# Attention value products with the transposed probabilities as stationary operand

## The chip, the cores and the metric

The kernel runs on one core of one Trainium2 chip. It is one launch, and the metric is the device time of that launch in microseconds (us). Five engines work in it, each through its own instruction queue in a fixed order: TensorE (PE; its weight loads are listed as PEld), VectorE (DVE), ScalarE (ACT), GpSimd (POOL) and SyncE (SP), which issues most of the DMA transfers.

## The reference, cut to what matters

The program is one inference step of a hybrid backbone with two layers, on 512 latent and 128 context tokens of 1024 features. Layer 0 mixes tokens with attention and RWKV-7 side by side, layer 1 with an S5 state space model; a SwiGLU stands before and after each mixer. The change touches attention alone, which computes for 8 query heads in 2 groups (one key and value head for each four of them), 64 features per head:

```python
def one_block(qblk):                     # 128 queries
    sc = jnp.einsum('bqkgd,btkd->bkgqt', qblk, k).astype(F32) * scale
    p = jax.nn.softmax(sc, axis=-1).astype(v.dtype)
    return jnp.einsum('bkgqt,btkd->bqkgd', p, v)
```

Latent queries read 640 keys (512 latent, 128 cached), context queries the 128 context keys.

## The kernel before, in words

Activations lie feature-major: features on partitions, tokens beside them. The five sub-layers outside the mixer of layer 0 do not change. In that mixer the input projection comes first, then the stage in question (`rwkv_attention`, L665), then the output projection (from L605 on).

In the stage four RWKV units of two heads each run one after the other: preparation (`rwkv_prep`, L939), inversion of triangular systems (`tri_inverse`), the chain of states from chunk to chunk (`rwkv_chain`, L1042) and the output (`rwkv_out`, L1140). They are generators; `take` (L679) draws from those of neighbouring units in turn and spreads 40 blocks of attention among them, so that the blocks fill gaps. This sets the order in which the program is written. A scheduler then orders the instructions of each engine by its own estimate of their times, so the order on an engine is not quite the written one.

A step of a chain is, on PE, a first product and one that adds the state (L1086, L1097), a copy of the result by ACT and DVE to `rt` (L1099), a product with it (L1102), a copy to `uv` (L1104), the next state (L1110, read out by DVE in L1113), and beside it what the tokens read (`ps_yr`, L1121 and L1123).

A block of attention (`att_block`, L896) is one query head and 128 queries. Four pairs of heads, five blocks of queries and two heads make 40 blocks: 32 with 640 keys, 8 with 128. In order:

- L905, L906 or L908 (PE): scores, queries on partitions, in the two wide banks of PSUM.
- L911, L912 (DVE): the row maximum, and its product with the scale.
- L914 (ACT): exponential into `att_p`, with the row sums beside it; L915 (DVE): one over the row sums.
- L916 (ACT): the probabilities times that, in place.
- L923 (PE): transposes of 128 by 128, five or one, into one or two PSUM banks `pt`; L925 (ACT): copies to `pts`, now with keys on partitions.
- L929 (PE): the value products, summed over the key tiles into the first of these banks. The values (`vt`, 64 columns of a head) are stationary, `pts` moves: 128 columns. The result has 64 features on partitions and 128 queries beside them, as the output projection wants it.
- L930 (ACT): copy to half of `att_out`; after the second head of a pair SP stores both heads with one DMA to `od` (L893).

PSUM tiles with the tag `ps` (scores excepted) come from three banks, given out in program order; `pt`, `ps_yr`, `ps_A`, `ps_hs` and others share them. All these products are in float32, and PE issues each as two passes (a transpose is one), with a weight load before each pass.

Of the kernel before, what the change touches and what calls it, by code (L numbers as in the profile page):

```python
# [18 lines left out]
LAT = 512  # L19
# [5 lines left out]
# token columns: latent 0..511, context 512..639; half 0 = 0..319, half 1 = 320..639  # L25
SEGS = (((0, HALF, 0),), ((0, LAT - HALF, 0), (LAT - HALF, HALF, 1)))
# weights are split ahead of this many instructions
# [4 lines left out]
class K:  # L32
    """The network on one core. Activations are feature-major: [features, tokens]."""
# [22 lines left out]
    def open_psum(self):  # L56
        """tags of PSUM and their buffers; a tag's buffers are given out in program order."""
        self.psum, self.banks = self.open("psum", 1, space=PSUM), {"ps": 3, "pn": 2, "pb": 1}
        # two banks side by side, for the mixer, and two more of ps otherwise
        self.wide = self.psum.tile([128, 1024], F32, name="ps_wide")  # L60
        self.five, self.count = True, 0

    def open_res(self):
        """temporaries, weights raw and in two parts, input of the next product, residual."""
        self.small = self.open("small", 2, "right")
        self.wraw = self.open("wraw", 3, "right")
        self.whl = self.open("whl", 4, "right")
        self.act = self.open("act", 1, "right")
        self.res = self.open("res", 1, "right")

    def load(self, dst, src):
        """a load that the scheduler keeps behind the load before it."""
# [28 lines left out]
    def setup(self):  # L101
        """parameters and tokens; the loads that the first sub-layer waits for come first."""
# [11 lines left out]
            # these wait until the first sub-layer runs  # L114
# [7 lines left out]
        def rows_of(name):  # L122
            """rows of parameters ..."""
# [11 lines left out]
        def columns(name, rows):  # L135
            """... turned into one scalar per partition."""
# [26 lines left out]
        # silu of both condition vectors; 32 stationary columns, of which 2 are in use  # L163
# [15 lines left out]
        # tokens, feature-major  # L179
# [10 lines left out]
        # the first sub-layer's vectors and norms  # L190
        self.ada(0, 0, ())
        self.new_h()
        for t in range(4):
            if t == 3:
# [3 lines left out]
                # 1 + the bias of scale; gain of the output times the weight of the residual  # L198
# [40 lines left out]
    def ada(self, l, j, parts):  # L239
        """pieces of work that make mods[l, j][:, part, d, group]: shift, scale, gate of sub-layer j of layer l."""  # L240
# [13 lines left out]
    def ada_piece(self, l, j, part, t, w=None):  # L254
        """two of the eight input tiles; four groups of 256 outputs go to as many column groups of the array."""
# [24 lines left out]
        if part:  # L280
            # gain * (1 + scale), or weight * gate * gain
            g = self.par["npre" if part == 1 else "npost"][:, i0:i0 + KT]
            nc.gpsimd.tensor_tensor(m[:, part], m[:, part], g[:, :, None].to_broadcast([128, KT, 2]), op=OP.mult)

# [1 line left out]
    def spill_x(self):  # L286
        """keep the residual in DRAM while a mixer needs the room."""
# [27 lines left out]
    def rms_bcast(self, ss):  # L315
        """ss [128, HALF]: squares summed over the feature tiles -> 1/rms on all partitions (PSUM)."""
        nc = self.nc
        ps = self.ps("ps_ms", "pn")
        # three blocks of 128 tokens; the last one overlaps, and its upper half counts
# [13 lines left out]
    def pre_norm(self, l, j, half, rb):  # L333
        """modulated input of sub-layer j as two float32r parts."""
# [35 lines left out]
    def post_norm(self, l, j, half, y, ssy, stats=True):  # L370
        """x += gate * rms_norm(y) * gain; returns the squares of x, summed over the feature tiles."""
# [16 lines left out]
    def wload(self, src, kt, n):  # L388
        """src: DRAM [kt*128, n] -> raw tile [128, kt, n]."""
# [4 lines left out]
    def wsplit(self, w, kt, c0, eng=None):  # L394
        """128 columns of a raw weight tile as two float32r parts."""
# [9 lines left out]
    def early_weights(self, l, j, between=None):  # L405
        """the first weights of a sub-layer, ready before its input: raw tiles and tiles in parts."""
# [14 lines left out]
    def mm3(self, ps, whl, acts, half, kt, k0=0, k1=None):  # L421
        """ps[:, :HALF] = sum over k of w[k]^T a[k], three passes; the terms k0 .. k1 of them."""
# [9 lines left out]
    def flush(self):  # L432
        """the norm of the second half, behind the first products of the first half."""
# [8 lines left out]
    def ffn(self, l, j, on_half, fillers=(), bg=()):  # L442
        """y[d][half] = swiglu(h); on_half(half, squares) when a half is complete."""
# [31 lines left out]
        def background():  # L475
# [3 lines left out]
            # behind the norms at the sub-layer's start  # L479
# [5 lines left out]
        for bi, (f0, f1) in enumerate(FBLOCKS):  # L485
# [9 lines left out]
            # the first and the last block take one half after the other, so that the norms of one half run  # L495
            # beside the products of the other
# [34 lines left out]
    def ab(self, l, j, on_half, fillers):  # L531
# [10 lines left out]
        def in_weights(c0, eng=None):  # L542
            """columns c0..c0+127 of the input projection."""
# [6 lines left out]
        def q_weights(i):  # L550
            """query heads i and 4 + i."""
# [28 lines left out]
        # the first products run beside the norm of the second half  # L580
# [16 lines left out]
        # what the last unit's output needs, and above it what is free before: even units, chains, the rest  # L597
# [9 lines left out]
        # output projection; its rows are permuted as the attention heads are  # L607
# [11 lines left out]
        # the place of the residual, which comes back when all of this is split  # L619
# [21 lines left out]
        # four products wait for the last unit's features only  # L641
# [23 lines left out]
    def rwkv_attention(self):  # L665
        """the units in turn: the chain of one runs beside the preparation of the next, and attention
        fills the gaps."""
        att = self.attention()
        # factors of a chunk's columns: block diagonal in the two heads
# [3 lines left out]
        # right sides of the chains' systems, over rows of zeros  # L673
# [5 lines left out]
        def take(rounds, n, *gens):  # L679
            """all of the generators, evenly, with n blocks of attention spread over them."""  # L680
# [58 lines left out]
    def ab_take(self, kind, n, half, ps):  # L739
        """one half of 128 projected features."""  # L740
        nc, mix = self.nc, self.mix
        if kind == "rw":
            # centred shift mix: (1 - mu) p + mu/2 (left + right)
# [41 lines left out]
        # mean square per token and head, tokens on partitions -> 1/rms  # L785
# [11 lines left out]
    def head_rsqrt(self, sq, scale, eps, op, name, bufs=2):  # L797
        """sq [128 = 2 heads x 64, NT] -> (scale * sums over a head  op  eps) ** -0.5 as [token, 5, 2]."""
# [12 lines left out]
    def head_bcast(self, st):  # L811
        """[token, 5, 2] -> [2 heads x 64, NT] in PSUM: (columns, their part)."""
# [12 lines left out]
    def mm_sq(self, lhsT, rhs, name):  # L825
        """[128, NT] = lhsT^T rhs in float32, in PSUM: (columns, their part)."""
# [6 lines left out]
    def rope(self, src, dst):  # L833
        """dst[:, :LAT] = src rotated; both [128, >= LAT]."""
# [29 lines left out]
    def att_values(self, v):  # L864
        """values with tokens on partitions: 4 latent blocks, the context, the cache."""
# [11 lines left out]
    def attention(self):  # L877
        """query heads i (rows 0..63) and 4 + i (rows 64..127), 128 queries at a time."""
        nc, mix = self.nc, self.mix
        # of both heads, each with zeros in place of the other's rows: the array's rows are all in use  # L880
# [3 lines left out]
        for i in range(4):  # L884
# [3 lines left out]
            for qb in range(5):  # L888
                o = self.mixe.tile([128, 128], F32, name="att_out", bufs=2)
                for kv in range(2):  # L890
                    self.att_block(qs[kv], self.attr[i], o, qb, kv)
                    if kv:
                        nc.sync.dma_start(self.od[i][:, qb * 128:(qb + 1) * 128], o)  # L893
                    yield

    def att_block(self, q, r8, o, qb, kv):  # L896
# [19 lines left out]
        nc.scalar.activation(p[:, :nk], p[:, :nk], AF.Identity, scale=mx[:, 3:4])  # L916
# [9 lines left out]
        po = pt[0][rows, :128]  # L926
        blocks = [0, 1, 2, 3, 5] if lat else [4]
        for n, b in enumerate(blocks):
            nc.tensor.matmul(po, self.vt[:, b, rows], pts[:, n], start=(n == 0), stop=(n == nkt - 1))  # L929
        nc.scalar.copy(o[rows], po)  # L930

# [1 line left out]
    # Unit i: heads 2i and 2i + 1, both directions, in chunks of 64 tokens. The backward direction  # L933
    # is the forward one on the reversed tokens; its chunks 0, 1 are the context, 2..9 latent.
    # Each stage is a generator, so that the stages of neighbouring units and attention take turns.
# [3 lines left out]
    def rwkv_prep(self, i, u):  # L939
        """decays, scaled factors and the products inside the chunks."""  # L940
# [10 lines left out]
        # normalised key direction, halved  # L951
# [13 lines left out]
        for d in range(2):  # L965
# [3 lines left out]
            # log decay: c1 * (tanh(z / 2) + 1), cumulated inside each chunk  # L969
# [43 lines left out]
            # rows: b | k of token s, columns: a | r of token t; and b | k with tokens on partitions  # L1013
# [21 lines left out]
        # bonus  # L1035
# [6 lines left out]
    def rwkv_chain(self, i, u):  # L1042
        """the states, chunk after chunk: four latent streams, and the four context streams beside them."""
        nc, I, O, mix = self.nc, self.I, self.O, self.mix
        am, v, ec = u["am"], u["v"], u["ec"]
        # values, tokens on partitions 64..127: position 0..7 latent chunks, 8, 9 context, per direction
# [852 lines left out]
```

## Time and profile before

| | us |
|---|---|
| three runs | 3339.91, 3347.76, 3350.36 |
| median | 3347.76 |
| span of the profiled execution, first to last instruction | 3337.1 |
| median less span (what lies around the span) | 10.7 |
| PE, DVE, ACT, POOL busy | 3091.3, 1923.3, 1210.2, 683.2 |
| the stage with attention: 738 to 1350 us of the span | 612 |

The span is read first by its share of busy time and its chain of waits, then by stretches: the stage is 18% of it, and nothing outside it is touched.

### The profile page before, as it was taken

Reading aid. Unit: us, or ns where it says so; the run is one execution under the profiler, and the core shown is the slowest. Engines: PE = TensorE matmul, PEld = TensorE weight load, DVE = VectorE, ACT = ScalarE, POOL = GpSimd, SP = SyncE. Lnnn points to the kernel's source line nnn. Section 1 sums busy time; section 2 is a strip of 40 time slices with the busy share of each in tenths; the row PEclk is TensorE's granted clock in tenths of the full one; section 3 lists DMA queues with packets and bytes.
Section 4 is the critical chain, followed back from the end, with each engine's and each line's share of the span. In section 5 each row is a group of like instructions: output and inputs, shape, how many; then the busy total and the mean of one; then the engine's idle time right before and its main releaser. Section 6 shows DMA issues by size and latency. Waiting matters only on the chain.

```text
span 3337.1 us, 55197 instructions
## 1 busy us (share of the span) xinstructions
PE 3091.3 (93%) x22259; PEld 2857.2 (86%) x22259; DVE 1923.3 (58%) x3731; ACT 1210.2 (36%) x2491; POOL 683.2 (20%) x795
## 2 busy tenths in 40 slices
PE   7999999986789789899999999999997689999998
PEld 6999998974576567789999999999996579999998
DVE  5433357428735861475466686666487955733346
ACT  4422235325334432453332453233353235422223
POOL 1000014132001200153333231233142533100002
PEclk8999999987778796899999999999998789999998
DMA  6433245620000000735443445454358863342223
GB/s 223 153 101 127 99 136 183 220 84 17 5 21 15 13 7 3 199 109 159 142 153 122 155 137 167 138 165 142 115 139 204 272 204 120 108 139 76 76 89 108
DMA packets 333924, 404.44 MB, mean 121 GB/s; under 512 B 42217, under 2 KB 299174, under 8 KB 333414
## 3 DMA queue, kind: packets, MB, share of 16 engines
q1 hardware_dynamic: 319174, 361.96, 34.4%
q0 software_dynamic: 14496, 38.97, 3.9%
q8 instruction: 175, 2.87, 0.4%
q14 instruction: 79, 0.65, 0.1%
HBM read 356.79 MB, written 42.89 MB: 120 GB/s over the span
## 4 chain that ended last, share of the span: by engine, by line
PE 80%; DVE 10%; issue 3%; POOL 2%; DMA 2%; ACT 2%; SPq 0%; POOLq 0%; DVEq 0%; ACTq 0%
PE ps_h L428 9%; PE ps_h L429 9%; PE ps_h L430 9%; PE ps_wide L428 5%; PE ps_wide L429 5%; PE ps_wide L430 5%; PE ps_y L428 5%; PE ps_y L430 5%; PE ps_y L429 5%; PE ps_wide L263 2%; PE ps_yr L1123 1%; PE ps_A L1020 1%; PE ps_pt L929 1%; PE ps_yr L1121 1%; DVE s5x L1564 1%
## 5 line engine op out<-in xcount | busy, mean ns | idle before, releaser
L401 DVE TENSOR_TENSOR wlo<-w,whi 128x1024 fp32r<-128x1024 f32 (+2 forms) x574 | 572.6, 1005 | 384.2 <-ACT whi L400 374.4
L400 ACT CAST whi<-w 128x1024 fp32r<-128x1024 f32 (+2 forms) x576 | 483.0, 847 | 857.0 <-PE ps_h L429 288.0
L428 PE MATMUL ps_h<-hh,whi 128*128 128x320 f32 x2112 | 658.0, 312 | 3.7 <-ACT hh L345 2.4
L429 PE MATMUL ps_h<-hl,whi 128*128 128x320 f32 x2112 | 656.7, 311 | 0.3 <-DVE hl L346 0.3
L430 PE MATMUL ps_h<-hh,wlo 128*128 128x320 f32 x2112 | 656.3, 311 | 0.0
L428 PEld LDWEIGHTS ps_h<-hh,whi 128*128 128x128 f32 x2112 | 399.2, 189 | 9.9 <-issue 3.4
L429 PEld LDWEIGHTS ps_h<-hl,whi 128*128 128x128 f32 x2112 | 398.8, 189 | 2.6 <-issue 1.5
L430 PEld LDWEIGHTS ps_h<-hh,wlo 128*128 128x128 f32 x2112 | 398.8, 189 | 1.1 <-issue 0.8
L429 PE MATMUL ps_y<-gl,whi 128*128 128x320 f32 x1056 | 325.8, 310 | 0.0
L430 PE MATMUL ps_y<-gh,wlo 128*128 128x320 f32 x1056 | 325.3, 310 | 0.0
L428 PE MATMUL ps_y<-gh,whi 128*128 128x320 f32 x1056 | 323.8, 311 | 1.1 <-ACT y L519 1.0
L428 PE MATMUL ps_wide<-hh,whi 128*128 128x320 f32 x912 | 288.6, 316 | 10.6 <-ACT y L653 4.4
L429 PE MATMUL ps_wide<-hl,whi 128*128 128x320 f32 x912 | 286.4, 314 | 1.3 <-DVE hl L346 1.2
L430 PE MATMUL ps_wide<-hh,wlo 128*128 128x320 f32 x912 | 285.3, 313 | 0.0
L362 POOL TENSOR_TENSOR ssy<-ssy,sq 128x320 f32<-128x320 f32 x84 | 96.0, 1142 | 566.1 <-ACT sq L361 563.5
L428 PEld LDWEIGHTS ps_y<-gh,whi 128*128 128x128 f32 x1056 | 197.1, 188 | 6.5 <-ACT y L519 2.2
L430 PEld LDWEIGHTS ps_y<-gh,wlo 128*128 128x128 f32 x1056 | 197.9, 188 | 1.0 <-issue 0.8
L429 PEld LDWEIGHTS ps_y<-gl,whi 128*128 128x128 f32 x1056 | 198.2, 188 | 0.7 <-issue 0.5
L428 PEld LDWEIGHTS ps_wide<-hh,whi 128*128 128x128 f32 x912 | 174.2, 191 | 17.9 <-issue 5.3
L470 DVE SCALAR_TENSOR_TENSOR g<-th,ps_h 128x320 f32<-128x320 f32 x159 | 77.0, 485 | 175.9 <-PE ps_h L430 175.3
L429 PEld LDWEIGHTS ps_wide<-hl,whi 128*128 128x128 f32 x912 | 173.7, 190 | 3.3 <-DVE hl L346 1.9
L430 PEld LDWEIGHTS ps_wide<-hh,wlo 128*128 128x128 f32 x912 | 173.6, 190 | 0.6 <-DVE wlo L401 0.3
(461 smaller groups left out, 5916.8 us busy)
## 6 DMA issues: line engine op xcount, KB each, us to landing
w<-in_ffn_w_dram SPq DMA_DIRECT2D x120, 1024.0 KB
ada_w<-in_ada_w_dram SPq DMA_DIRECT2D x72, 1024.0 KB
w<-in_ffn_w_dram SPq DMA_DIRECT2D x112, 512.0 KB
w<-in_ab_w_in_dram SPq DMA_DIRECT2D x14, 1024.0 KB
s5cd<-s_work POOLq DMA_DIRECT2D x128, 64.0 KB, 2.4
s5bd<-s_st POOLq DMA_DIRECT2D x32, 256.0 KB, 3.1
s5bt<-s5bd SPq DMA_DIRECT2D x32, 256.0 KB
w<-in_s_w_out_dram SPq DMA_DIRECT2D x8, 1024.0 KB
```

Source lines behind the costliest of these rows:

```text
L263: nc.tensor.matmul(ps[32 * g:32 * g + 32, :256], self.sc[:, 2 * t + k, :], w[:, k, g * 256:g * 256 + 256], start=(t + k == 0), stop=(2 * t ...
L362: nc.gpsimd.tensor_tensor(ss, ss, sq, op=OP.add)
L400: a = self.nc.scalar.copy(hi[:, :kt], s)
L401: v = (eng or self.nc.vector).tensor_tensor(lo[:, :kt], s, hi[:, :kt].bitcast(F32), op=OP.subtract)
L428: nc.tensor.matmul(o, hi[:, k], ah[k][half], start=(k == 0), stop=False)
L429: nc.tensor.matmul(o, hi[:, k], al[k][half], start=False, stop=False)
L430: self.last[0] = nc.tensor.matmul(o, lo[:, k], ah[k][half], start=False, stop=(k == kt - 1))
L470: nc.vector.scalar_tensor_tensor(g, t, 0.5, p3[:, :HALF], op0=OP.mult, op1=OP.mult)
L929: nc.tensor.matmul(po, self.vt[:, b, rows], pts[:, n], start=(n == 0), stop=(n == nkt - 1))
L1020: nc.tensor.matmul(pA[:, j % 2 * 256:j % 2 * 256 + 256], bk[:, j].rearrange("p a t -> p (a t)"), arb[:, j].rearrange("p h a t -> p (h a t) ...
L1121: nc.tensor.matmul(py[hr, col(d)], uv[:, d, p, h], rv(am[:, d, p, h, 64:]), start=True, stop=first)
L1123: nc.tensor.matmul(py[hr, col(d)], s[hr, d, p], rv(u["ar"][d][hr, self.chunk(d, p), 1]), start=False, stop=True)
```

## The change

The probabilities stay undivided: L916 goes. They are transposed as before, but in the value products they are now the stationary operand (128 by 128), and the values move (64 columns), so that the result has queries on partitions and the 64 features of the head beside them. There the row sums lie on partitions too, and the copy out of PSUM divides by them (an activation with a scale per partition, 128 by 64, in place of the copy of 64 by 128). The two heads of a pair fill the columns of one tile `att_o`. After the second head this tile is transposed by PE into the second quarter of the bank that the block's value products used, ACT copies it to `att_out`, and the same DMA stores it. `att_o` and `att_out` have one buffer each; before, `att_out` had two. In the changed file lines from L893 on stand 4 or 5 lines further down, and comments are gone. The core of the diff:

```diff
             for qb in range(5):
-                o = self.mixe.tile([128, 128], F32, name="att_out", bufs=2)
+                o = self.mixe.tile([128, 128], F32, name="att_o", bufs=1)
                 for kv in range(2):
-                    self.att_block(qs[kv], self.attr[i], o, qb, kv)
+                    ps = self.att_block(qs[kv], self.attr[i], o, qb, kv)
                     if kv:
-                        nc.sync.dma_start(self.od[i][:, qb * 128:(qb + 1) * 128], o)
+                        ot = self.mixe.tile([128, 128], F32, name="att_out", bufs=1)
+                        nc.tensor.transpose(ps[:, 128:256], o, self.ident)
+                        nc.scalar.copy(ot, ps[:, 128:256])
+                        nc.sync.dma_start(self.od[i][:, qb * 128:(qb + 1) * 128], ot)
                     yield
...
         nc.vector.reciprocal(mx[:, 3:4], mx[:, 2:3])
-        nc.scalar.activation(p[:, :nk], p[:, :nk], AF.Identity, scale=mx[:, 3:4])
...
-        po = pt[0][rows, :128]
+        po = pt[0][:, :64]
         blocks = [0, 1, 2, 3, 5] if lat else [4]
         for n, b in enumerate(blocks):
-            nc.tensor.matmul(po, self.vt[:, b, rows], pts[:, n], start=(n == 0), stop=(n == nkt - 1))
-        nc.scalar.copy(o[rows], po)
+            nc.tensor.matmul(po, pts[:, n], self.vt[:, b, rows], start=(n == 0), stop=(n == nkt - 1))
+        nc.scalar.activation(o[:, rows], po, AF.Identity, scale=mx[:, 3:4])
+        return pt[0]
```

How this moves instructions shows at three places. The first is on ACT, where the first unit's chain starts: `uv<-ps_v` are copies of transposed values for the chain, `inv_x` and `s_hist` belong to the RWKV units too. Before:

```order
L914 ACTIVATE att_p,mx<-ps_wide,mx,rms_q 128x640
L1061 COPY uv<-ps_v 64x256 x2
L930 COPY att_out<-ps_pt 64x128
L1061 COPY uv<-ps_v 64x256 x2
L1183 COPY inv_x<-inv_a 128x1024
L916 ACTIVATE att_p<-att_p,mx 128x640
L1061 COPY uv<-ps_v 64x256 x6
L1072 COPY s_hist<-ps_s_8084 128x2x64
```

The same place on ACT now:

```order
L918 ACTIVATE att_p,mx<-ps_wide,mx,rms_q 128x640
L1066 COPY uv<-ps_v 64x256 x2
L934 ACTIVATE att_o<-ps_pt,mx 128x64
L1066 COPY uv<-ps_v 64x256 x2
L1188 COPY inv_x<-inv_a 128x1024
L1066 COPY uv<-ps_v 64x256 x6
L1077 COPY s_hist<-ps_s_8087 128x2x64
```

The scaling of the probabilities no longer stands ahead of the six copies and of `s_hist`; all else kept its order.

The second place is on PE, in a step of the first unit's chain with a block of attention beside it (`ps_c` are the chain's products, `keys` the scores, `pts` the value products). Before:

```order
L929 MATMUL ps_pt<-pts,vt 64x128 x5
L1090 MATMUL ps_c_8389<-s_hist,ident 128x128
L905 MATMUL ps_wide<-keys,att_qin_7296 128x512
L906 MATMUL ps_wide<-keys,att_qin_7296 128x128
L1102 MATMUL ps_c_8387<-rt_7220,am 64x64 x2
L1102 MATMUL ps_c_8388<-rt_7220,am 64x64 x2
L1110 MATMUL ps_c_8389<-uv,bt 64x64 x2
L1121 MATMUL ps_yr<-am,uv 64x64
L1123 MATMUL ps_yr<-ar,s_hist 64x64
L923 MATMUL ps_pt<-ident,att_p 128x128 x5
```

The same step on PE now:

```order
L933 MATMUL ps_pt<-vt,pts 128x64 x5
L1095 MATMUL ps_c_8395<-s_hist,ident 128x128
L909 MATMUL ps_wide<-keys,att_qin_7296 128x512
L910 MATMUL ps_wide<-keys,att_qin_7296 128x128
L1107 MATMUL ps_c_8393<-rt_7220,am 64x64 x2
L1107 MATMUL ps_c_8394<-rt_7220,am 64x64 x2
L895 MATMUL ps_pt<-ident,att_o 128x128
L1115 MATMUL ps_c_8395<-uv,bt 64x64 x2
L1126 MATMUL ps_yr<-am,uv 64x64
L1128 MATMUL ps_yr<-ar,s_hist 64x64
L926 MATMUL ps_pt<-ident,att_p 128x128 x4
```

The new transpose (L895) came in between the chain's third product and the product that waits for the copy of it (L1115); the block of attention kept its place in the step.

The third place is the end of the stage on PE, where the last block's value product is followed by the last unit's group norm (`gn_sq`). Before:

```order
L1134 MATMUL ps_fin<-ident,s_fin 64x128 x2
L923 MATMUL ps_pt<-ident,att_p 128x128
L829 MATMUL ps_cen<-yb,k_cmat 128x384
L829 MATMUL ps_cen<-yb,k_cmat 128x256
L929 MATMUL ps_pt<-pts,vt 64x128
L802 MATMUL ps_hs<-k_hsel,gn_sq 128x2 x5
```

The same on PE now:

```order
L1139 MATMUL ps_fin<-ident,s_fin 64x128 x2
L926 MATMUL ps_pt<-ident,att_p 128x128
L829 MATMUL ps_cen<-yb,k_cmat 128x384
L829 MATMUL ps_cen<-yb,k_cmat 128x256
L933 MATMUL ps_pt<-vt,pts 128x64
L895 MATMUL ps_pt<-ident,att_o 128x128
L802 MATMUL ps_hs<-k_hsel,gn_sq 128x2 x5
```

The transpose of the last pair came in ahead of the sums of the group norm.

## Rows read from the trace of the kernel before

**Rows 1.** Stretches: length; PE, PEld, DVE, ACT, POOL busy (instructions); clock, DMA, GB/s.

```profile
738.00:858.00 120.00, 80.54 (x305) 54.62 (x305) 93.51 (x159) 56.66 (x101) 28.51 (x17) 0.70 0.05 15
738.00:1350.00 612.00, 513.99 (x3752) 384.50 (x3752) 351.46 (x724) 226.89 (x515) 71.20 (x42) 0.78 0.04 12
```

**Rows 2.** Chain of waits, 738:1350: share of the stretch by line.

```profile
by line: PE ps_yr L1123 6.7%; PE ps_A L1020 6.6%; PE ps_pt L929 6.0%; PE ps_yr L1121 5.7%; PE ps_c L1102 4.5%; PE ps_wide L905 4.4%; PE ps_c L1086 4.3%; DVE inv_a L1180 4.2%; DVE am L1199 3.7%; issue 3.6%; PE ps_c L1110 3.6%; PE ps_c L1097 
```

**Rows 3.** Groups by shape, 738:1350: busy us, mean ns | idle before, releaser.

```profile
L929 PE MATMUL ps_pt<-pts,vt 128*64 128x128 f32 x336 | 57.0, 321 | 9.1 <-ACT pts L925 9.1
L916 ACT ACTIVATE att_p<-att_p,mx 128x640 f32<-128x640 f32 x32 | 26.5, 828 | 24.3 <-DVE mx L915 24.0
L925 ACT COPY pts<-ps_pt 128x128 f32<-128x128 f32 x40 | 10.7, 267 | 12.0 <-PE ps_pt L923 12.0
L916 ACT ACTIVATE att_p<-att_p,mx 128x128 f32<-128x128 f32 x8 | 3.2, 400 | 6.2 <-DVE mx L915 6.1
```

**Rows 4.** Chain in order of time: start us, us, PE passes.

```profile
769.99 1.24 PE ps_pt L929 x10
...
802.62 2.24 PE ps_hs L802 x10
...
957.25 2.13 PE ps_pt L929 x10
...
1091.63 1.28 PE ps_hs L802 x10
```

**Rows 5.** Timeline, first unit's chain: start us, us, instruction [idle, releaser].

```profile
887.74 0.82 ACT L916 ACTIVATE att_p<-att_p,mx 128x640 f32<-128x640 f32 x1
...
889.00 0.41 PE L1057 MATMUL ps_v<-ident,v_rev 128*64 128x128 f32 x2 [2.21 <-ACT uv L1061]
...
907.27 0.68 PE L1102 MATMUL ps_c<-rt,am 128*64 128x64 f32 x8
```

**Rows 6.** Timeline, the third unit's chain.

```profile
1192.52 0.83 ACT L916 ACTIVATE att_p<-att_p,mx 128x640 f32<-128x640 f32 x1
...
1194.61 0.49 PE L1090 MATMUL ps_c<-s_hist,ident 128*128 128x128 f32 x2 [0.66 <-ACT s_hist L1072]
```

**Rows 7.** Timeline, the end of the stage.

```profile
1349.32 0.33 SPq L893 DMA_DIRECT2D od<-att_out  x1
...
1349.69 3.96 SPq L73 DMA_DIRECT2D w<-in_ab_w_out_dram  x6
```

**Rows 8.** Chain of waits behind that.

```profile
1353.04 6.99 DMA w<-in_ab_w_out_dram
```

**Rows 9.** Timeline of DVE, read-outs of the last unit's states.

```profile
1283.91 0.29 DVE L1113 TENSOR_TENSOR s_hist<-ps_c,ec 128x128 f32<-128x128 f32 x1 [0.54 <-PE ps_c L1110]
...
1287.82 0.29 DVE L1113 TENSOR_TENSOR s_hist<-ps_c,ec 128x128 f32<-128x128 f32 x1 [0.54 <-PE ps_c L1110]
...
1329.47 0.29 DVE L1113 TENSOR_TENSOR s_hist<-ps_c,ec 128x128 f32<-128x128 f32 x1 [1.60 <-PE ps_c L1110]
...
1337.04 0.29 DVE L1113 TENSOR_TENSOR s_hist<-ps_c,ec 128x128 f32<-128x128 f32 x1 [1.59 <-PE ps_c L1110]
```

**Rows 10.** Stretch of the last unit.

```profile
1291.00:1345.00 54.00, 52.05 (x328) 40.22 (x327) 8.84 (x29) 5.23 (x17) 1.97 (x1) 0.50 0.00 1
```

**Rows 11.** Stretches around runs of value products.

```profile
956.40:959.70 3.30, 3.30 (x18) 2.85 (x17) 0.29 (x1) 0.26 (x1) 0.00 (x0) 0.50 0.00 0
959.80:966.40 6.60, 6.49 (x90) 4.99 (x89) 1.74 (x6) 1.09 (x3) 0.00 (x0) 1.00 0.00 0
...
1256.70:1260.00 3.30, 3.30 (x19) 2.95 (x20) 0.36 (x2) 0.40 (x1) 0.00 (x0) 0.50 0.00 0
1260.20:1263.40 3.20, 3.20 (x91) 2.95 (x89) 0.00 (x0) 1.65 (x4) 0.00 (x0) 1.00 0.00 0
```

**Rows 12.** Timeline of PE, transposes of the input tokens.

```profile
7.56 2.77 PE L184 MATMUL ps_xin<-ident,xin 128*128 128x128 f32 x12
...
10.90 1.47 PE L184 MATMUL ps_xin<-ident,xin 128*128 128x128 f32 x12
```

## The prediction, as it was put on record before the result

> **What bounds the kernel now.** I read the stretches first, since the change touches one stage only, 738 to 1350 us, 612 of the 3337.1 us of the span. Over the stage PE is busy for 514 us, DVE for 351, ACT for 227 [rows 1]. ACT is idle for 63% of it, so that work taken off ACT counts only where somebody waits for ACT. In the preparation of the first unit, 738 to 858 us, DVE leads with 93.5 of 120 us and PE has 80.5 [rows 1]; behind that PE leads. The chain of waits says the same by line: the long entries are PE products, with some DVE transposes of the inversions between them, and no line of ACT is among those shown [rows 2]. The value products (L929) have 6.0% of the stage on that chain, 36.7 us [rows 2], of their 57.0 us of busy time [rows 3]: 64% of what they cost lies on the path. I use 0.64 as the rate at which PE work of the attention blocks turns into time.
>
> **What goes on ACT.** 32 scalings of 828 ns and 8 of 400 go, 29.7 us, and with them 30.3 us in which ACT stood still in front of them, waiting for the reciprocal from DVE [rows 3]. The reciprocal stays, but the copy that needs it now comes a whole group of PE work later. What comes is 20 copies of 128 by 128, 267 ns each by the like copy of `pts` [rows 3], 5.3 us, hidden by ACT's idle time; without that cover they would cost the 5.3 us. The copy out of PSUM keeps its number (40).
>
> Where did PE wait for that scaling? Not for the scaled probabilities: the transposes stand so late on PE that none of their idle time is put down to L916. It waits where something else was queued behind it on ACT. The largest is at 889 us: the scaling begins at 887.74 and takes 0.82, the copies for the chain come behind it, and PE idles 2.21 us for them [rows 5], of which the scaling explains at most its own 0.82 us. Another is at 1194.6 us, 0.66 us [rows 6]. There are a dozen such places; counting at each the smaller of PE's wait and the scaling's duration they add to 4.3 us. The order on ACT at 889 us is now the same without the scaling, so the next thing that is late there is the product that feeds the copies. Bounds: 0 and -4.3; I take -4, since the two largest waits stand in stretches that PE leads.
>
> **What the swap costs PE.** A pass had 64 stationary and 128 moving columns; it has 128 and 64 now, so the product of both is the same. No product of this shape is in the trace. The nearest rows bound it from both sides. With 128 stationary columns and only 2 moving ones (L802) ten passes took 1.28 us at the full clock and 2.24 at the half one; the value products took 1.24 and 2.13 [rows 4]. So the load of a full stationary operand by itself sets a pace as slow as today's. With 64 and 64 (L1102) eight passes took 0.68 us [rows 5], which is 0.85 for ten. I take the first: the stationary side is what the two have in common. There are 33.6 groups of ten passes (336), and at the stage's mean granted clock of 0.78 [rows 1] 44% of the time is at the half level: 33.6 x (0.56 x 0.04 + 0.44 x 0.11) = 2.4 us, on the path 1.5.
>
> **What the new transposes cost.** 20 passes of 128 by 128 at today's pace of the value products, 0.124 or 0.213 us [rows 4]: 3.3 us, at 0.64 2.1. But the scheduler put them, as in the chain step shown, behind the third product, where the next one has to wait for a copy by ACT or DVE anyway. I take half, 1.0 us; bounds 0 and 3.3. A transpose waits for the division on ACT; what is queued behind it on PE is the chain. The bank `pt` is held until the copy behind the transpose; the next user of that bank comes some four products later, so I put nothing for it, 20 times 0.6 us (a pass, a copy and the way between them) if all of it showed. The store waits for the copy too, and the single buffer of `att_out` for the store before; there are 20 stores in 612 us, so this should hide.
>
> **The end of the stage.** Here there is no cover. The last pair's store is issued at 1349.32, and behind it in SP's queue are the six loads of the output weights, from 1349.69 on [rows 7]; the chain of waits goes through them into a load that takes 6.99 us [rows 8]. The store now waits for one transpose (0.12) and one copy (0.27) more, with two handovers: +0.6 us.
>
> **The sum.** 1.5 + 1.0 + 0.6 - 4 = -0.9 us. The profiled execution has a span of 3337.1 us, and the median of the runs lies 10.7 above it; I keep that distance: 3337.1 - 0.9 + 10.7 = 3346.9, so 3347 us, beside a median of 3347.76. A difference under 0.3%, 10 us, can't be told from none here; the three runs alone are 10 us apart.
>
> **Rival 1: the moving columns set the pace.** Then the value products run as L1102 does, 0.85 instead of 1.24 us for ten, and 31% of their 36.7 us go: -11.5, and the 1.5 of the swap with it: 3334 us. For it speaks that L1102 is the only row with so few moving columns beside a real product; against it L802, whose two moving columns bring no speed at all. [...]
>
> **Rival 2: the clock stays up in the last unit's chain.** It runs at the granted clock of 0.50 from 1291 to 1345 us [rows 10]. A step takes 7.57 us there and took 3.91 just before, at the full level [rows 9]. If the clock stays up, 54 us shrink by 26, to 3321; if it comes back midway, by 13, to 3334, which I take as this case's time. It fell after a few waits of PE, and small shifts could spare it. Against it: this unit has almost no attention beside it, so the change reaches it only through the two last context blocks.
>
> **Rival 3: slower, the clock rises less often.** Five times in the stage the clock rises just as a run of value products at the half level ends: at 959.7 (after the run of 957.25), 983.6, 1017.7, 1239.6 and 1260.1 us; the first and the last pair of stretches are shown, 0.50 and then 1.00 [rows 11]. The stretches at full clock behind the five add to 70.6 us. With half the moving columns such a run may not lift the clock any more, and PE stays slow until the next dense work, scores or `ps_A`. If a third of the 70.6 us is lost, 23.5 us take 1.94 times as long [rows 9], +22, and at the rate of 0.64 +14: 3361 us; all of it would be +42. The change turns slower as soon as some 16 us of full clock go, half a stretch like that from 983.6 on. Against it: the other 18 rises of the stage do without a run of value products, a run still keeps PE occupied as long, and 20 transposes are added. [...]
>
> **How the numbers follow.** The forecast 0.60, rival 1 0.06, rival 2 0.15, rival 3 0.19. The forecast's own bounds are 3343 (all of the 4.3 gained, nothing lost) and 3356 (nothing gained, transposes in full, half of the bank's price), with the scatter of the runs 3338 to 3358, which is within 0.3%. Rivals 1 and 2 are faster, 0.21 together, rival 3 slower, 0.19, the forecast no change, 0.60. The range of 3330 to 3364 holds the forecast, rival 1, the nearer half of rival 2 and the nearer part of rival 3; about 1 in 10 is left out on either side.
>
> **What would show it.** In the profile after: ten passes of L933 at 1.28 us at full clock and 2.24 at half (near 0.85: rival 1). ACT busy in the stage down by some 24 us, while PE's busy time grows by 3 to 6. The wait at 889 us shorter by up to 0.8 us. The last store about 0.6 us later behind its value product, and the weights' loads with it. The mean granted clock of the stage near 0.78: above 0.82, with the last chain at the full level, is rival 2; below 0.74, with no rise behind runs of L933, rival 3. The forecast is wrong if the stage's length moves by over 10 us, and its reasons are wrong if that happens with clock and pass times as today, that is, if an idle time on PE that I have not listed goes or comes, above all one in front of the first transpose of a block, for the bank.

## The result, and the profile after

| | before | changed |
|---|---|---|
| median of 5 runs, us | 3347.76 (3339.91 to 3350.36) | 3362.84 (3361.66 to 3371.45) |
| ratio, 95% interval | | 1.0051 [1.0034, 1.0068] |
| second series, median of 28 and 11 runs | 3344.50 | 3351.72 |
| ratio, 95% interval | | 1.0025 [1.0014, 1.0036] |
| profiled span, us | 3337.1 | 3359.9 |

The change made the kernel slower, by 0.5% in the first series and by 0.25% in a second one of the same code; the forecast was no change. The step that failed is the clock: the sum kept the stage's granted clock as it was and put nothing for rises that might be lost, and rival 3, which had them lost, got 0.19. In the profile after, the clock rises 18 times in the stage, where the prediction counted 23.

The stretches after (length; busy time and instructions of PE, PEld, DVE, ACT, POOL; granted clock; DMA share, GB/s). The first line is the whole stage, the next three one piece of it that is cut at a run of value products:

```profile
738.00:1366.00 628.00, 527.57 (x3776) 402.27 (x3776) 348.60 (x726) 206.46 (x495) 73.53 (x43) 0.75 0.04 12
1227.30:1243.90 16.60, 11.87 (x75) 9.17 (x75) 9.11 (x12) 2.15 (x6) 0.00 (x0) 0.50 0.00 0
1244.00:1246.20 2.20, 2.20 (x12) 2.20 (x11) 0.00 (x0) 0.00 (x0) 0.00 (x0) 0.50 0.00 0
1246.40:1288.60 42.20, 42.20 (x352) 35.23 (x353) 4.39 (x17) 11.19 (x33) 2.23 (x1) 0.50 0.03 7
```

The same piece before:

```profile
1229.50:1239.50 10.00, 7.71 (x48) 6.37 (x49) 7.85 (x9) 2.15 (x6) 0.00 (x0) 0.50 0.00 0
1239.70:1249.80 10.10, 9.65 (x144) 7.97 (x143) 2.23 (x8) 2.58 (x6) 0.00 (x0) 1.00 0.03 8
```

ACT lost 20 us of busy time against [rows 1], 227 to 206, where 24 were forecast. PE's busy time grew by 13.6 us and not by 3 to 6, with more of it at the half level: the mean clock fell from 0.78 to 0.75. Most of that is one place: before, the run of value products that ends at 1239.5 was followed at once by the full level; now the run of the same block, 1244.0 to 1246.4, leaves the clock at 0.50, and PE is busy without a gap for another 42 us at that level. No rise follows the next run at 1267.6 either, for another 18 us.

What this costs is read off the updates of the state by DVE, which mark the steps of the third unit's chain. Before, the update ahead of the place, the second one behind that and the first of the next unit's chain (start, us, instruction, idle time before it):

```profile
1221.23 0.29 DVE L1113 TENSOR_TENSOR s_hist<-ps_c,ec 128x128 f32<-128x128 f32 x1 [0.43 <-PE ps_c L1110]
...
1239.87 0.29 DVE L1113 TENSOR_TENSOR s_hist<-ps_c,ec 128x128 f32<-128x128 f32 x1 [1.58 <-PE ps_c L1110]
...
1279.37 0.28 DVE L1113 TENSOR_TENSOR s_hist<-ps_c,ec 128x128 f32<-128x128 f32 x1
```

The same updates after:

```profile
1220.52 0.29 DVE L1118 TENSOR_TENSOR s_hist<-ps_c,ec 128x128 f32<-128x128 f32 x1 [0.20 <-PE ps_c L1115]
...
1241.28 0.29 DVE L1118 TENSOR_TENSOR s_hist<-ps_c,ec 128x128 f32<-128x128 f32 x1 [2.86 <-PE ps_c L1115]
...
1294.85 0.28 DVE L1118 TENSOR_TENSOR s_hist<-ps_c,ec 128x128 f32<-128x128 f32 x1
```

Up to 1221 us the changed profile is 0.7 us ahead. Over the piece it takes 74.3 us in place of 58.1: 16.2 us lost. Of these, 2.1 are lost up to the second update; after the change that update comes before the run at 1244.0, so the run has no part in them. 14.1 come behind it.

The value products and the new instructions (group; busy us, mean ns, idle time before):

```profile
L933 PE MATMUL ps_pt<-vt,pts 128*128 128x64 f32 x336 | 55.1, 313 | 6.6 <-ACT pts L928 6.5
L934 ACT ACTIVATE att_o<-ps_pt,mx 128x64 f32<-128x64 f32 x40 | 12.6, 315 | 42.0 <-PE ps_pt L933 41.6
L895 PE MATMUL ps_pt<-ident,att_o 128*128 128x128 f32 x20 | 6.8, 342 | 0.5 <-ACT att_o L934 0.5
L896 ACT COPY att_out<-ps_pt 128x128 f32<-128x128 f32 x20 | 5.3, 267 | 12.9 <-PE ps_pt L895 12.9
```

And three entries of the chain of waits (start, us, ten passes each), two at the full level and one at the half one:

```profile
988.32 1.21 PE ps_hs L802 x10
...
1202.68 1.26 PE ps_pt L933 x10
...
1244.07 2.33 PE ps_pt L933 x10
```

A pass keeps its pace although half as many columns move, as the row of L802 had said [rows 4]. The transposes are released by the division and wait 0.5 us in all.

The end of the stage, chain of waits:

```profile
1364.72 0.34 PE ps_pt L895
1365.06 0.02 issue
1365.08 0.28 ACT att_out L896
1365.36 0.02 issue
1365.38 0.33 SPq L897
...
1369.10 8.71 DMA w<-in_ab_w_out_dram
```

One transpose, one copy and the handovers between are 0.66 us; 0.6 was forecast. The store is 16.1 us later than in [rows 7]. The load behind it took 8.71 instead of 6.99 us [rows 8], and the span ends 22.8 us later. Of the 6.7 us beyond the store, 1.7 are this load; 6.5 come between some 2500 and 2720 us (201.5 us where it took 195.0), in code that the change does not touch, and a little is won back elsewhere. So the two profiles lie further apart than the medians.

### The profile page after: what moved, and what is told of

Its sections match the earlier page's. It is cut to its first block, busy times and chain, and to the rows that moved or that the text cites. A ratio compares the mean times of both kernels' runs of the same rounds, so it can differ in the third digit from the quotient of the medians.

```text
span 3359.9 us, 55254 instructions
## 1 busy us (share of the span) xinstructions
PE 3102.3 (92%) x22279; PEld 2874.1 (86%) x22279; DVE 1919.0 (57%) x3731; ACT 1193.7 (36%) x2471; POOL 687.0 (20%) x795
## 4 chain that ended last, share of the span: by engine, by line
PE 81%; DVE 9%; DMA 3%; issue 2%; POOL 2%; ACT 2%; SPq 0%; POOLq 0%; DVEq 0%; ACTq 0%
PE ps_h L428 9%; PE ps_h L429 9%; PE ps_h L430 9%; PE ps_wide L428 5%; PE ps_wide L429 5%; PE ps_wide L430 5%; PE ps_y L428 5%; PE ps_y L429 5%; PE ps_y L430 5%; PE ps_wide L263 2%; PE ps_A L1025 2%; PE ps_yr L1128 1%; PE ps_yr L1126 1%; PE ps_pt L933 1%; DVE s5x L1569 1%
```

## The experiments

In each series the kernels ran on one chip with the kernel before (medians 3345.73, 3345.41 and 3344.50 us). "Clock" is the mean over the span and over a kernel's runs; before has 0.930, the changed kernel 0.925 in its second series. Each kernel has one profile, so what is read at a place is read from one execution of it.

**128 moving columns.** The moving operand takes both heads' values; the copy out picks the block's half.

```diff
-        po = pt[0][:, :64]
+        po = pt[0][:, :128]
-            nc.tensor.matmul(po, pts[:, n], self.vt[:, b, rows], ...)
+            nc.tensor.matmul(po, pts[:, n], self.vt[:, b], ...)
-        nc.scalar.activation(o[:, rows], po, AF.Identity, scale=mx[:, 3:4])
+        nc.scalar.activation(o[:, rows], po[:, rows], AF.Identity, scale=mx[:, 3:4])
```

> The changed kernel, but each value product moves all 128 columns of the values (both heads of the group; the copy out takes the 64 that belong to the block). Theory A (a run of value products with only 64 moving columns no longer lifts TensorE's clock): the clock of the stage comes back from 0.74 to about 0.78 and the time to 3340 to 3350 us, since a pass is paced by its weight load anyway (ten passes at 1.25 to 1.35 us). Rival B (the new order, the transposes of the outputs or the division at the end cost the 15 us, not the columns): time stays at 3360 to 3368 us, or grows by some 2 us for the longer passes.

Measured: 3336.78 us, 0.9976 [0.9966, 0.9986] of before, clock 0.933. The place that went wrong:

```profile
1239.40:1249.40 10.00, 8.14 (x45) 6.65 (x45) 7.41 (x9) 2.15 (x6) 0.00 (x0) 0.50 0.00 0
1249.60:1256.20 6.60, 6.09 (x84) 5.05 (x84) 1.65 (x6) 1.10 (x4) 0.00 (x0) 1.00 0.05 12
```

The run there (1247.16, 2.48 us) is followed by the full level again. The result is even faster than theory A said. The place alone doesn't explain that: in this profile the piece takes 64.4 us, less than the 74.3 of the changed kernel but more than the 58.1 of before. The last unit's chain, from its first update of the state to its last, takes 51.0 us, where it took 57.7 before and 55.8 in the changed kernel.

**The kernel before without the scaling** (the division is left out):

```diff
-        nc.scalar.activation(p[:, :nk], p[:, :nk], AF.Identity, scale=mx[:, 3:4])
```

> The kernel before without the scaling of the probabilities (the division is left out altogether). Prices the gain on ScalarE alone. By the forecast's term: 4 us faster, 3342 to 3346 us, clock of the stage near 0.78. Rival (the shifted work meets the clock's steps otherwise, with no change of the products): a change of more than 8 us in either direction, with a clock that moved and pass times as before.

Measured: 3334.51 us, 0.9961 [0.9947, 0.9975], clock 0.933. That is 11 us, and not the 4 of the forecast's term. It is what the rival named: the products are as before, and the clock moved all the same. What of it is the scaling's own is worked out below.

**The changed kernel without the output transposes:**

```diff
-                        ot = self.mixe.tile([128, 128], F32, name="att_out", bufs=1)
-                        nc.tensor.transpose(ps[:, 128:256], o, self.ident)
-                        nc.scalar.copy(ot, ps[:, 128:256])
-                        nc.sync.dma_start(self.od[i][:, qb * 128:(qb + 1) * 128], ot)
+                        nc.sync.dma_start(self.od[i][:, qb * 128:(qb + 1) * 128], o)
```

(`att_o` has two buffers here.)

> The changed kernel without the transposes of the outputs and their copies (the outputs are stored with queries on partitions, so what follows computes with misplaced numbers). Theory A: still slow, 3357 to 3365 us, clock of the stage 0.73 to 0.75, since the value products are unchanged. Rival B (the transposes and the waits for their bank cost it): back to 3340 to 3348 us.

Measured: 3345.48 us, 1.0000 [0.9988, 1.0012], clock 0.930: in rival B's range and 12 us under theory A's. By the time alone theory A would fall. The profile says otherwise: at the disputed place the clock stays down as in the changed kernel,

```profile
1218.00:1275.90 57.90, 53.21 (x421) 44.35 (x422) 13.46 (x29) 11.04 (x32) 2.23 (x1) 0.50 0.02 4
```

and the piece takes 73.1 us, 1.2 less than in the changed kernel's first profile. The time was made up elsewhere: 9.8 us ahead of the place, and some 10 in the last chain and behind it, where the clock rose at 1323.8 us. So a median could not settle it; a place could.

**The kernel before with 128 stationary columns** (both heads' values stationary, 128 columns moving as before):

```diff
-        po = pt[0][rows, :128]
+        po = pt[0][:, :128]
-            nc.tensor.matmul(po, self.vt[:, b, rows], pts[:, n], ...)
+            nc.tensor.matmul(po, self.vt[:, b], pts[:, n], ...)
-        nc.scalar.copy(o[rows], po)
+        nc.scalar.copy(o[rows], po[rows])
```

> The kernel before, with both heads' values (128 columns in place of 64) as stationary operand and only the block's half copied out; 128 columns move as before. If the clock goes by moving columns alone: clock near 0.78, time 3347 to 3353 us (up to 2 us for the larger weight load). If it goes by the product of rows, columns and moving columns: these products count twice, clock above 0.80 and time below 3340 us.

Measured: 3344.10 us, 0.9990 [0.9978, 1.0001], clock 0.930, as before. Twice the stationary columns changed neither time nor clock.

**128 moving columns in two blocks only, and in all but these two.** They are the two blocks whose runs stand in the slow piece.

```diff
+        self.nblk = getattr(self, "nblk", -1) + 1
+        cols, wide = (slice(0, 128), rows) if self.nblk in (35, 36) else (rows, slice(0, 64))
...
-            nc.tensor.matmul(po, pts[:, n], self.vt[:, b, rows], ...)
+            nc.tensor.matmul(po, pts[:, n], self.vt[:, b, cols], ...)
```

(For the complement `not in`. The slices of `po` that go with it are left out.)

> The changed kernel, with 128 moving columns in the value products of two blocks only: those whose runs of ten passes, at 1244 and 1268 us in the profile after, stand in the 61 us at the half level. Theory A (64 moving columns do not lift the clock, 128 do): the clock rises behind one or both of these two runs, 10 to 20 us shorter, 3343 to 3355 us. Rival B (the transposes of the outputs, or the shift of the work, keep the clock low there): no rise behind the two runs and a time within 5 us of the changed kernel's 3363.

Measured: 3341.27 us, 0.9986 [0.9974, 0.9999] of before, under the expected range. In its profile the clock follows that of the changed kernel almost step by step up to 1227 us, then:

```profile
1227.00:1247.30 20.30, 15.43 (x95) 12.33 (x95) 9.24 (x12) 2.46 (x7) 0.00 (x0) 0.50 0.00 0
1247.50:1254.20 6.70, 6.58 (x108) 5.59 (x109) 1.64 (x6) 1.92 (x5) 0.00 (x0) 1.00 0.05 12
```

So the first of the two runs is followed by a rise. The second is not, although it moves 128 columns too. It comes in two parts, and the half level lasts another 15 us behind it:

```profile
1263.26 2.08 PE L935 MATMUL ps_pt<-vt,pts 128*128 128x128 f32 x8
1265.27 0.70 PE L1104 MATMUL ps_c<-s_hist,ar 64*64 64x64 f32 x8
1265.90 0.79 PE L935 MATMUL ps_pt<-vt,pts 128*128 128x128 f32 x2
```

```profile
1254.40:1281.40 27.00, 27.00 (x220) 22.34 (x219) 2.74 (x11) 6.99 (x21) 2.22 (x1) 0.50 0.03 6
```

The piece takes 69.1 us, 5.2 less than in the changed kernel:

```profile
1220.40 0.29 DVE L1120 TENSOR_TENSOR s_hist<-ps_c,ec 128x128 f32<-128x128 f32 x1 [0.20 <-PE ps_c L1117]
...
1289.54 0.28 DVE L1120 TENSOR_TENSOR s_hist<-ps_c,ec 128x128 f32<-128x128 f32 x1
```

> The complement: 128 moving columns in all blocks but these two, which keep 64. Against the kernel with 128 in all (3337 us): theory A expects no rise behind these two runs and 6 to 15 us more, 3343 to 3352 us. Rival B: the same 3337 us within 4.

Measured: 3348.08 us, 1.0017 [0.9998, 1.0036], 11 us above the kernel with 128 everywhere, and the slow piece is back:

```profile
1240.30:1294.80 54.50, 51.87 (x407) 43.08 (x408) 12.38 (x28) 12.06 (x35) 2.23 (x1) 0.50 0.02 5
```

Here the piece takes 70.9 us, 6.5 more than with 128 columns everywhere. The twelve runs fall into two groups, eight from 3341 to 3349 us and four from 3361 to 3369, and the profile is one of the four; the eight have no profile.

Two blocks of 40, altered one way or the other, move the rise behind the first run, and the piece by 5 to 6.5 us. That is about a third of the 16.2 us. The profiled spans differ by more, 22.4 us (changed and two blocks 128) and 18.1 us (all 128 but two, and all 128); the larger part of that comes from other places, such as the last unit's chain (51.0 us with the shorter spans, 55.8 and 56.5 with the longer).

**The scaling kept, in the changed kernel and with 128 moving columns:** L916 comes back, and the copy out is a plain copy.

> The changed kernel with the scaling of the probabilities kept and a plain copy in place of the division at the end (same result). ScalarE gets its 30 us back. If taking the scaling off gave what the kernel before without it showed (11 us), this is 8 to 14 us slower than the changed kernel, 3371 to 3377 us; by the forecast's term 4 us, 3365 to 3369; if the clock decides alone, no difference beyond 3 us.

Measured: 3353.39 us, 1.0019 [1.0007, 1.0030], clock 0.926, under all three ranges, which had been set from the first series' 3363. Beside the 3351.72 of the second series, "no difference beyond 3 us" is nearest.

> 128 moving columns in all value products, the scaling of the probabilities kept and a plain copy in place of the division at the end. The scaling's price where the clock comes up: by the forecast's term 4 us, so 3340 to 3342; by what the kernel before showed without it (11 us), 3346 to 3350; if it is hidden, 3335 to 3338.

Measured: 3348.99 us, 1.0013 [0.9999, 1.0027], clock 0.929 against 0.933: 12 us more than without the scaling. By the time that is the second of the three ranges; how much of it is the clock is worked out below.

**The changed kernel once more.**

> The changed kernel once more, on the same chip as the three beside it, for a base with more runs than five. Expected near its first median, 3355 to 3368 us, with a mean clock of 0.921 to 0.925 over the span; in the profile no rise of the clock behind its value products around 1244 and 1268 us.

Measured: 3351.72 us, below the expected range, clock 0.925. The slow piece is there, 1223.1 to 1280.9 us at 0.50. The same code is 11 us apart in the two series; by the slope worked out below, some 6 of these go with the clock (0.922 and 0.925).

**128 moving columns without the transposes** (edit as above).

> 128 moving columns in all value products, without the transposes of the outputs and their copies (outputs stored with queries on partitions, so what follows computes with misplaced numbers). The transposes' price where the clock does come up: by the forecast's term 1 us (bounds 0 and 3), so 3334 to 3337 us. If the transposes cost what leaving them out gave in the changed kernel (17 us): 3318 to 3322.

Measured: 3345.17 us, 1.0004 [0.9994, 1.0013]: 8 us slower than with the transposes, at a clock of 0.9285 against 0.933. Both expectations had it as fast or faster.

**Products without a reader in the last chain**, on top of 128 moving columns, first two in each step, then eight in one step:

```diff
+            if i == 3 and not first:
+                for k in range(2):
+                    nc.tensor.matmul(self.wide[:, 640 + 128 * k:768 + 128 * k], self.ident, s[:, :, p], start=True, stop=True)
...
+            if i == 3 and p == 2:
+                for k in range(8):
+                    kc = 640 + k % 2 * 128
+                    nc.tensor.matmul(self.wide[:, kc:kc + 128], self.ident, s[:, :, p], start=True, stop=True)
```

> 128 moving columns in all value products, and in the last unit's chain two products of 128 by 128 by 128 without a reader in each step, where PE waits 0.3 to 0.4 us for a copy. If the columns moved decide the clock, the last chain stays at the full level for most of its 75 us: a step of 4 to 5 us in place of 7.5, 15 to 25 us less than the 3337 of the kernel without them, 3312 to 3322. If the clock is set by something else: a few us slower, 3338 to 3342.

Measured: 3347.75 us, 1.0018 [1.0003, 1.0033], slower than both expectations. The clock stayed down through the chain, with PE busy all the time, and a step took 8.3 us (1330.27 to 1338.53) in place of 7.6:

```profile
1289.20:1347.00 57.80, 57.80 (x350) 45.76 (x350) 9.46 (x35) 6.31 (x21) 1.97 (x1) 0.50 0.00 1
```

> 128 moving columns in all value products, and in one step of the last unit's chain (the fifth), where the clock has just fallen, eight products of 128 by 128 by 128 without a reader, some 3.4 us at the half level. If a dense run of 128 moving columns lifts the clock as a run of the value products does, the steps behind it take 4 to 5 us in place of 7.5 for some 20 us: 3 to 12 us less than 3337 (in a part of the runs the clock comes up later in this chain anyway), 3325 to 3334. If not: 3 us slower, 3340.

Measured: 3321.59 us, 0.9939 [0.9921, 0.9958]: the fastest of all, 23 us under before and under the expected range. One of the six runs, 3338.97 us at a clock of 0.935, did not gain. The run in PE's timeline:

```profile
1292.04 3.78 PE L1108 MATMUL ps_wide<-s_hist,ident 128*128 128x128 f32 x16
```

The stretches ahead of its end and behind it:

```profile
1290.40:1297.00 6.60, 6.60 (x35) 5.80 (x33) 0.67 (x3) 0.77 (x2) 1.97 (x1) 0.50 0.00 0
1297.20:1334.50 37.30, 33.97 (x331) 26.11 (x330) 10.38 (x37) 7.35 (x25) 0.39 (x1) 1.00 0.04 13
```

Thirty-six passes spread over nine steps, twelve of them ahead of the fall, were followed by no rise; sixteen in one run were followed by 37 us at the full level. What rival 2 hoped would happen by itself was bought for 3.8 us. The waits of PE that rival 2 put ahead of the fall are in the profile before, four of 0.17 to 0.35 us from 1274.3 to 1281.5 us. But the fall at 1290.8 comes behind 6.8 us in which PE was busy for 6.77, so that waits bring it is not shown.

## Why the prediction was wrong

**The clock, where it failed.** "With half the moving columns such a run may not lift the clock any more" is what happened; I gave it 0.19, and 0.60 to a sum that keeps the clock as it was. My grounds against it were that a run still keeps PE occupied as long, and that other rises do without such runs. The first does not count: in the slow piece PE is busy 42.2 of 42.2 us and the clock stays at 0.50. The second is true and beside the point, since at this place no other work was followed by a rise for 42 us. The rival had the clock stay down until the next scores or `ps_A`. In the profile before, 17 of the 18 other rises do have one of these in the 3 us ahead of them; in the slow piece after, the scores at 1247.5 and 1276.2 us were followed by none, and the rise at 1288.7 comes as ten products of L1062 end (1286.89, 2.13 us). The stage's mean clock came to 0.75, just above the mark of 0.74 that I had set for this rival; the place told more than the mean. The first run of value products in the third unit's slow piece, in all profiles:

| kernel | moving columns there | rise after the run's end, us | half level around it, us |
|---|---|---|---|
| before | 128 | 0.1 | 10.2 |
| before, no scaling | 128 | 0.4 | 3.4 |
| before, 128 stationary | 128 | 2.5 | 20.5 |
| all 128 | 128 | -0.2 | 10.2 |
| two blocks 128 | 128 | 1.1 | 20.5 |
| all 128, no transposes | 128 | 2.2 | 20.5 |
| all 128, scaling kept | 128 | 1.3 | 23.9 |
| all 128, two in each step | 128 | 0.2 | 10.2 |
| all 128, burst | 128 | 0.2 | 10.2 |
| changed | 64 | 42.3 | 61.4 |
| changed, again | 64 | 39.9 | 58.0 |
| changed, no transposes | 64 | 38.9 | 58.0 |
| changed, scaling kept | 64 | 40.9 | 58.0 |
| all 128 but two blocks | 64 | 44.4 | 54.6 |

Nine to five without an exception, over kernels that differ in transposes, scaling and stationary columns. (In the kernel before without the scaling the fall itself comes at the run.) The kernel before has the same product of stationary and moving columns as the changed one, and its run is followed by the rise; so of the shape it is the moving side that the rise follows here.

The table shows one place, and it is no rule for the stage. At the next block's run, four of the kernels with 128 moving columns were at the half level: in two the clock rose while it ran (before; all 128), in two it stayed down for 15 us more (two blocks 128; all 128, scaling kept). With 64 columns it stayed down in all five. Near 984 us a run of 64 columns is followed by the full level too, 1.8 us after its end, in the changed kernel with the scaling kept. So 128 moving columns did not always bring the rise, and 64 were not always without one; what else decides is open, and so is whether the other four rises named in rival 3 went by the columns.

**The size.** The rival took a third of 70.6 us as lost and came to 14 us, 3361. The piece lost 16.2, and the first series ended at 3362.84. That nearness is in part luck. Between the same two updates 61.4 us stand at the half level where 23.9 did. The 37.5 us more are, as an estimate, 19.3 us of work at the full level (1.94 times, [rows 9]); so 18.2 us were to be lost, and 16.2 were, a rate of 0.89. The rival had more full level lost, 23.5 us, at a lower rate, 0.64. The columns of the two blocks account for 5.2 us of the piece, with all blocks at 128 for 9.9 (74.3 to 64.4); the rest of the 16.2 is not explained by an experiment. In the second series the change cost 7 us. The scatter goes with the clock: within the runs of one kernel, the span falls by 1.84 us for each 0.001 of mean clock (227 runs of 13 programs, each series against its own mean; correlation -0.81). The last chain is part of this. Six transposes stand in it; PE's timeline of the changed kernel:

```profile
1332.36 1.65 PE L821 MATMUL ps_hb<-ident,xb 128*128 128x128 f32 x6
```

The same with 128 columns everywhere, and that kernel's stretch behind them:

```profile
1333.48 1.56 PE L821 MATMUL ps_hb<-ident,xb 128*128 128x128 f32 x6
```

```profile
1334.90:1358.60 23.70, 19.42 (x186) 14.70 (x184) 6.55 (x20) 4.48 (x14) 1.84 (x1) 1.00 0.09 30
```

The same six, and in the first case the clock stayed at 0.50 behind them, up to 1363.7. In four profiles the clock rises as they end (all 128; two blocks 128; all 128, scaling kept; changed, no transposes), in nine it does not, and in the burst's it was up already. These four go with either number of moving columns in the value products. So a row of transposes can be what stands before a rise. Two such rows stand at the program's start too, the second at nearly twice the pace of the first [rows 12], but no rise is shown there: the granted clock is given as 1.00 for 6.00 to 10.70 us as well as for 10.90 to 15.00. Why the nine differ is not settled, and so is whether the 20 added transposes could speak against rival 3.

**The swap on PE, +1.5:** right in kind, and smaller. Ten passes at 1.26 and 2.33 where 1.28 and 2.24 were forecast; whole runs at the half level take 2.39 us before (at 981.36) and 2.40 after (at 975.81). Rival 1, which needed 0.85 at the full level, is out: ten passes of L933 still take 1.26 with 64 moving columns.

**ACT, -4:** not refuted, but not shown. (The time ACT stood still for the reciprocal adds to 30.1 us in [rows 3], not 30.3; nothing hangs on it.) I compare mean spans and take out the clock by the slope above. All 128: 12.0 us more with the scaling, of which 7.1 are clock: 4.9. The kernel before without it: 12.1 less, 5.1 of them clock: 7.0. The changed kernel: 2.9 less with the scaling, 1.0 of it clock: -1.9. On average 3.3, with a spread as large, so that neither its size nor its sign is settled. The wait that I named at 889 us is gone: PE waits 0.39 us there, at 888.5, for `s_hist`, where it waited 2.21 [rows 5]. That is more than the 0.8 us that the scaling was to explain.

**The transposes, +1:** likewise. Without them the changed kernel's mean span is 8.8 us shorter, of which the clock explains 9.5; with 128 columns it is 7.8 longer, and the clock explains 8.8. Nothing beyond 1 us is left either way. Whether the transposes or only the shift of the work moved the clock in these two is not settled; the opposite signs would fit the shift.

**The base.** I held the 10.7 us between the profiled span and the median for something around the span. It is scatter: in every run with both numbers the time is 1.7 to 2.1 us above the span (3361.66 and 3359.9 in the profiled one after), so the profiled execution of before was an early finisher. This did not decide the sign.

## What to carry to other kernels

Where PE's granted clock changes inside a stage, look at what PE did just before each rise, and count a change to that instruction as a change to the clock: an edit that leaves the time of a pass alone was followed by 42 us more at the half level at one place, and the piece took 16 us longer. Where a pass takes as long with fewer moving columns, as here (ten passes 2.40 us with 64 and 2.48 with 128), moving more of them costs little, and here it paid, though half the result is thrown away. Medians that differ by 8 us through the clock say little about a small edit; compare the same place across several profiles, compare times at equal clock, and add up the other places before the whole difference is put down to one.

## What the runs showed of the hardware that was not expected

- A busy PE was not always followed by a rise: it was busy 57.8 of 57.8 us at a granted clock of 0.50, while 3.8 us of products of 128 moving columns in one run, in the same chain, were followed by 37 us at 1.00.
- A product of 128 by 128 by 128 took hardly longer than one with 64 moving columns: ten passes 2.48 and 2.40 us at the half level.
- A row of six transposes, or a run of value products, of the same shape and length was followed by a rise in some profiles and not in others (four of thirteen for the transposes), so one place in one profile does not give a rule.
- Doubling the stationary columns (64 to 128) at 128 moving ones changed neither pace nor mean clock (0.930): 57.4 us for 334 passes in the stage, against 57.0 for 336 before.
